# Dealing 90 adaLN steps differently over a two-layer hybrid block

## The chip, the core and the metric

The kernel runs on one core of a Trainium2 chip. Its engines go by the profile's names: PE multiplies matrices (PEld loads its weights), DVE, ACT and POOL do elementwise work, SP issues all transfers from HBM. The metric is the device time of one execution in microseconds, as the median of several runs. All arithmetic is float32; products are made from a high and a low float32r part of both operands, in three matmuls.

## The reference

Two layers over 256 latent tokens and 256 context tokens of width 1024. Per layer six adaLN vectors of 1024 (shift, scale and gate for the mixer, then for the feed forward) are products of a conditioning vector with a 1024 x 6144 matrix, one set per stream:

```python
mod_x = (jax.nn.silu(c) @ w_ada[l] + b_ada[l])[:, None, :]
mod_c = (jax.nn.silu(c_ctx) @ w_ada[l] + b_ada[l])[None, None, :]
shift1, scale1, gate1, shift2, scale2, gate2 = jnp.split(mod_x, 6, axis=-1)
...
hx = modulate(x, shift1, scale1)          # LN(x) * (1 + scale) + shift
mix_x, _ = token_mixer(hx, *mixer_w, rope, ctx_kv)
x = layer_norm(alpha * x + gate1 * mix_x, ln1_g[l], ln1_b[l])
ffn_x = swiglu(modulate(x, shift2, scale2), w_up[l], w_down[l])
x = layer_norm(alpha * x + gate2 * ffn_x, ln2_g[l], ln2_b[l])
```

The mixer is attention, a gMLP and a Fourier branch, merged under three sigmoid gates (`merged = sum of gate_b * (branch_b @ P_b)`) and multiplied with `w_out`. The last layer needs its context stream for keys and values alone, so of its context vectors only shift1 and scale1.

## The kernel before, in words

**Order of the work.** The code does not issue instructions itself. Every operation is appended to a plan in program order (its rank). Buffers are then given out in program order, each from a ring of its class: 7 `raw` tiles of 128x1024 for arriving weights, 3 `whi` and 3 `wlo` for their two parts, 34 `A` tiles, 8 PSUM banks. Last, a list scheduler with costs and latencies written into the code (`cost`, `LATENCY`) puts the operations of each engine in a fixed order: an engine that is free takes the ready operation of lowest rank. On the chip every engine goes through its own list strictly in order and waits where the next operation is not ready.

**A weight tile.** `load_w` transfers 512 KB into a `raw` tile, ACT copies it to `whi` (rounded), DVE subtracts it to get `wlo`; a resident tile goes to `A` tiles instead (`rhi`, `rlo`). The raw tile is free after the subtraction.

**An adaLN step.** `ada_queue` holds closures; `ada_step(n)` takes the next n. A tile step (`ada_tile`) loads 128 columns of `w_ada` (512 KB, one raw tile) and for each stream issues one DVE SCALAR_TENSOR_TENSOR (tile `junkv`) that multiplies by the broadcast conditioning row and sums into one column of `mod`; a small accumulator read follows. A group of six per layer (0 shift1, 1 scale1, 2 gate1, 3 shift2, 4 scale2, 5 gate2) is eight tile steps and one `fin` step (`ada_fin`), which adds the bias. For gates 2 and 5 `fin` also transposes on PE (`gtp`), copies on ACT (`grw`) and writes the gate to DRAM, from where it is read back as a broadcast row (`grow`).

**The stages.** Layer 0 carries both streams, 512 tokens. In the mixer the blocks of `w_in` come first (`zp`), with attention in the background; then for each of eight feature tiles j the three gates (`gp`, three weight tiles, 72 matmuls) of tile j+1 and the merge (`bp`, two weight tiles, 48 matmuls) of tile j, and after each merge some adaLN steps and, in the last layer, `after_merge`, which preloads `w_out`. Then `w_out` (`pj`), normalisations, the feed forward's up projection (`up`, feature tiles j = 0 to 21: the first three by `up_tile`, the rest by `up_seven`, a Strassen-like scheme with seven products of 12 matmuls), the down projection (`proj_streams`, k = 0 to 21, adaLN steps after each of the first 16), and layer 1 with 256 tokens in the same order, with `w_up_tok` (`ut`) at the start of its up projection.

**up_seven.** Each j takes two raw tiles for its weights and two more (`upy`, `upz`) for sums that DVE makes. DVE also evacuates the products; among these `nc.vector.tensor_tensor(f[:, 0], f[:, 0], a, op=ALU.subtract)` (tile `upf`) reads bank `a`, into which the next product `t4` accumulates.

**Who needs what when.** Layer 0's groups 2 to 5 are used in layer 0 after the merges. Layer 1's groups 0 and 1 are used when layer 1 begins, group 2 after its merges, 3 and 4 in its `mod`, 5 at the end. Before, 36 steps lay in layer 0's merges (5 each for four, 4 each for four), 26 in the down projection (2 each for ten, 1 each for six), 28 in layer 1's merges (4 each for four, 3 each for four). The queue has 32 tile steps of layer 0 with two streams, 16 of layer 1 with two (groups 0, 1), and 32 of layer 1 with one.

Of the kernel before, what the change touches and what calls it, by code (L numbers as in the profile page):

```python
# [39 lines left out]
RATE = [0.38, 0.5]  # L40

KEEP = 5

SPARE = 24

# [261 lines left out]
class Builder:  # L307
# [208 lines left out]
        else:  # L516
            nc.vector.tensor_tensor(m, m, b, op=ALU.add)

    def ada_enqueue(self, l, g, streams):
        for j in range(8):  # L520
            self.ada_queue.append(lambda j=j: self.ada_tile(l, g * 8 + j, streams))
        def fin():
            for s in streams:
                self.ada_fin(l, g, s)
        self.ada_queue.append(fin)

    def ada_step(self, n=1):
        for _ in range(n):
# [524 lines left out]
    def mixer(self, l, hx, hx_tiles, hc, early, pre=None, after={}, after_merge=None):  # L1053

        nc, io = self.nc, self.io
        both = l == 0
        streams = [0, 1] if both else [0]
# [114 lines left out]
        own, g = {}, []  # L1172
# [13 lines left out]
        for j in range(8):  # L1186
            if j < 7:
                self.gates(l, j + 1, hx, N, g, own)
                self.bg_drain()
            if j % 2 == 0:  # L1190
                for s in streams:
                    o, ts = self.feats(2, 256, f"mT{s}{j}")
                    mT[s] += o
                    mt[s] += ts
            self.merge(l, j, [g.pop(0) for _ in range(3)], own, A["aT"], gT, fT, N, [mT[s][j] for s in streams])
            self.ada_step((5 if both else 4) if j < 4 else (4 if both else 3))
            if after_merge:
                after_merge(j)
        return mT, mt
# [5 lines left out]
    def run(self):  # L1205
# [84 lines left out]

        for g in (2, 3, 4, 5):
            self.ada_enqueue(0, g, [0, 1])
        for g in (0, 1):
            self.ada_enqueue(1, g, [0, 1])
        for g in (2, 5, 3, 4):
            self.ada_enqueue(1, g, [0])


        mT, mt = self.mixer(0, hT, ht, None, early, pre)
# [20 lines left out]
        for s in range(2):  # L1320
            y = ys[s]
            done = lambda i, b: y.__setitem__(i, self.gated(b, grow[s]))
            if s == 0:
                held = self.proj_pair(io["w_out"][0], range(KD), mT[0], done, range(KD - KEEP, KD))
            else:
                order = [(k - KEEP) % KD for k in range(KD)]
                self.proj_pair(io["w_out"][0], order, mT[1], done, (), held, during_ctx)
# [6 lines left out]
        def hid_alloc(j):  # L1334
            if j % 2 == 0:
                t = self.a_tile([128, 2, 2, 2, 128], F32, f"hid{j}")
                hid.extend(t[:, i] for i in range(2))
# [11 lines left out]
        for j in range(NH, KF):  # L1349
            hid_alloc(j)  # L1350
            self.up_seven(j, h2, S, hid[j])

        ln = self.ln_rows(0, 1)
        hn, hnt = [None, None], [None, None]
# [3 lines left out]
        def down_done(s, i, b):  # L1358
# [4 lines left out]
            if (s, i) == (1, 0):  # L1363
# [1 line left out]
                self.modulated(y[0], 1, 0, 0, hn[0], 0)  # L1365

        self.proj_streams(io["w_down"][0], KF, hid, down_done, 6,
                          lambda k: self.ada_step(2 if k < 10 else 1))


        def ctx_in():
# [156 lines left out]
```

## Time and profile before

| | |
|---|---|
| time, median of 3 runs | 1324.29 us (1322.74 to 1325.91) |
| profiled execution, its own time | 1327.01 us |
| its span, first to last instruction | 1325.2 us |
| mean granted PE clock | 0.991 |
| adaLN tile steps | 128 instructions of 1233 ns on DVE, 157.8 us |

Shares are of the span. PE's busy time is modelled from the length of each matmul, so that a matmul that waits for nothing can still come more slowly; the pace (start to start) says more. The granted clock is a share of 2.4 GHz.

### The profile page before, as it was taken

How to read it: one execution, taken by the hardware profiler on the slowest of the kernel's cores; microseconds unless marked ns; L12 is line 12 of the kernel's file. 1: busy time of each engine (PE TensorE's matmuls, PEld its weight loads, DVE VectorE, ACT ScalarE, POOL GpSimd, SP SyncE). 2: the span in 40 equal slices, each digit the busy share in tenths (PEclk: the TensorE clock that was granted, in tenths of full speed). 3: DMA queues.
4: the chain of work that ended last, by engine and by line, in shares of the span. 5: the costliest groups of instructions: out<-in, count | busy, mean ns of one | idle time of the engine just before them, and what ended most of it. 6: DMA issues, size and time to landing. Idle time of an engine off the chain costs nothing.

```text
span 1325.2 us, 20495 instructions
## 1 busy us (share of the span) xinstructions
PE 1299.6 (98%) x7878; PEld 1150.5 (87%) x7878; DVE 1020.7 (77%) x1878; ACT 608.2 (46%) x1080; POOL 96.2 (7%) x99
## 2 busy tenths in 40 slices
PE   9999999999999999999999999999999899999997
PEld 8887888888888889999999888878899897799985
DVE  6867886876786679688989996786987787766665
ACT  4456564332222446455556323564754453444450
POOL 0032100000100111000000000242000001100000
PEclk8999999999999999999999999999999899999999
DMA  9611115445455730133336786044257795555551
GB/s 367 238 48 48 48 60 160 143 142 175 160 184 182 286 127 33 49 98 111 112 99 221 259 281 237 27 145 138 89 179 246 260 331 209 178 187 184 187 191 48
DMA packets 60819, 214.29 MB, mean 162 GB/s; under 512 B 7297, under 2 KB 8113, under 8 KB 60721
## 3 DMA queue, kind: packets, MB, share of 16 engines
q1 hardware_dynamic: 60720, 212.98, 47.9%
q8 instruction: 62, 1.02, 0.3%
q14 instruction: 37, 0.30, 0.1%
HBM read 211.88 MB, written 1.07 MB: 161 GB/s over the span
## 4 chain that ended last, share of the span: by engine, by line
PE 85%; DVE 6%; DMA 4%; ACT 2%; issue 2%; POOL 0%; SPq 0%; DVEq 0%; ACTq 0%; POOLq 0%
PE up L295 24%; PE pj L295 18%; PE zp L295 15%; PE gp L295 11%; PE bp L295 7%; DMA raw<-in_w_ada_t 3%; PE pvp L295 2%; PE sp L295 2%; PE tpp L295 1%; DVE junkv L295 1%; PE adp L295 1%; PE ut L295 1%; DVE wlo L295 1%; PE trp L295 1%; DMA raw<-in_w_out 1%
## 5 line engine op out<-in xcount | busy, mean ns | idle before, releaser
L295 ACT ACTIVATE whi<-raw 128x1024 fp32r<-128x1024 f32 x216 | 228.5, 1060 | 345.6 <-issue 97.3
L295 DVE TENSOR_TENSOR wlo<-raw,whi 128x1024 fp32r<-128x1024 f32 x216 | 264.2, 1225 | 132.7 <-ACT whi L295 132.2
L295 DVE SCALAR_TENSOR_TENSOR junkv<-raw,silb 128x1024 bf16<-128x1024 f32 x128 | 157.8, 1233 | 32.0 <-DMA raw<-in_w_ada_t 30.5
L295 PE MATMUL up<-h,whi 128*128 128x256 f32 x880 | 155.2, 281 | 0.0
L295 PEld LDWEIGHTS up<-h,whi 128*128 128x128 f32 x880 | 133.8, 189 | 0.2
L295 PE MATMUL up<-h,wlo 128*128 128x256 f32 x440 | 120.6, 281 | 0.0
L295 PE MATMUL gp<-hT,whi 128*128 128x512 f32 x384 | 120.3, 394 | 0.0
L295 PE MATMUL zp<-whi,hT 128*128 128x512 f32 x320 | 111.7, 404 | 0.1
L295 PEld LDWEIGHTS gp<-hT,whi 128*128 128x128 f32 x384 | 71.6, 188 | 15.4
L295 PEld LDWEIGHTS up<-h,wlo 128*128 128x128 f32 x440 | 81.6, 188 | 0.0
L295 PE MATMUL pj<-whi,hidp 128*128 128x512 f32 x256 | 79.8, 392 | 0.0
L295 PE MATMUL gp<-hT,wlo 128*128 128x512 f32 x192 | 75.7, 394 | 0.0
L295 PE MATMUL gp<-hx,whi 128*128 128x256 f32 x384 | 73.5, 290 | 2.0 <-ACT whi L295 2.0
L295 PEld LDWEIGHTS zp<-whi,hT 128*128 128x128 f32 x320 | 60.2, 190 | 12.0 <-DVE hT L295 0.5
L295 ACT ACTIVATE rhi<-raw 128x1024 fp32r<-128x1024 f32 x44 | 45.6, 1054 | 47.2 <-DMA raw<-in_w_out 19.8
L295 PE MATMUL zp<-whi,hx 128*128 128x512 f32 x192 | 66.1, 407 | 0.2 <-ACT moda L295 0.2
L295 DVE TENSOR_TENSOR rlo<-raw,rhi 128x1024 fp32r<-128x1024 f32 x44 | 54.5, 1246 | 14.7 <-ACT rhi L295 14.6
L295 PEld LDWEIGHTS gp<-hx,whi 128*128 128x128 f32 x384 | 61.9, 197 | 2.4 <-ACT whi L295 2.2
L295 PE MATMUL zp<-wlo,hT 128*128 128x512 f32 x160 | 63.3, 397 | 0.0
L295 PE MATMUL bp<-aT,whi 128*128 128x512 f32 (+1 forms) x256 | 63.1, 338 | 0.0
L295 PE MATMUL gp<-hx,wlo 128*128 128x256 f32 x192 | 55.6, 290 | 1.9 <-DVE wlo L295 1.9
L295 POOL TENSOR_TENSOR gth<-gth 128x512 f32<-128x512 f32 (+1 forms) x16 | 24.2, 1510 | 455.7 <-DVE gth L295 302.1
(291 smaller groups left out, 3165.5 us busy)
## 6 DMA issues: line engine op xcount, KB each, us to landing
raw<-in_w_ada_t SPq DMA_DIRECT2D x80, 512.0 KB, 4.4
raw<-in_w_up SPq DMA_DIRECT2D x80, 512.0 KB, 3.7
raw<-in_w_in_tok SPq DMA_DIRECT2D x48, 512.0 KB, 4.0
raw<-in_w_gate SPq DMA_DIRECT2D x48, 512.0 KB, 4.4
raw<-in_w_down SPq DMA_DIRECT2D x44, 512.0 KB, 3.9
raw<-in_w_br SPq DMA_DIRECT2D x32, 512.0 KB, 3.7
raw<-in_w_out SPq DMA_DIRECT2D x19, 512.0 KB, 5.9
wsh<-in_w_ada_s SPq DMA_DIRECT2D x8, 512.0 KB, 10.7
```

Source lines behind the costliest of these rows:

```text
L295: getattr(getattr(nc, eng), method)(*map(real, args), **{k: real(a) for k, a in kw.items()})
```

## The change

Steps move; their number (90) and the work of each stay. `ADA_MERGE` gives layer 0's merges 6,6,6,6,6,5,5,5 steps (45) and layer 1's 2,2,1,1,1,1,1,1 (10). A step is added after every odd j of `up_seven` from 3 to 17 (8), and the down projection has 27. The queue is put in another order: layer 1's group 0 goes to the end of layer 0's merges; the eight tiles of its group 2 go to the feed forward, without their `fin`; groups 1, 3 and 4 go to the down projection; `fin` of group 2 stays the first step of layer 1's merges, and group 5 follows it.

```diff
+ADA_MERGE = [[6, 6, 6, 6, 6, 5, 5, 5], [2, 2, 1, 1, 1, 1, 1, 1]]
...
-    def ada_enqueue(self, l, g, streams):
-        for j in range(8):
-            self.ada_queue.append(lambda j=j: self.ada_tile(l, g * 8 + j, streams))
-        def fin():
-            for s in streams:
-                self.ada_fin(l, g, s)
-        self.ada_queue.append(fin)
+    def ada_enqueue(self, l, g, streams, tiles=True, fin=True):
+        if tiles:
+            for j in range(8):
+                self.ada_queue.append(lambda j=j: self.ada_tile(l, g * 8 + j, streams))
+        if fin:
+            self.ada_queue.append(lambda: [self.ada_fin(l, g, s) for s in streams])
...
-            self.ada_step((5 if both else 4) if j < 4 else (4 if both else 3))
+            self.ada_step(ADA_MERGE[l][j])
...
-        for g in (0, 1):
-            self.ada_enqueue(1, g, [0, 1])
-        for g in (2, 5, 3, 4):
+        self.ada_enqueue(1, 0, [0, 1])
+        self.ada_enqueue(1, 2, [0], fin=False)
+        self.ada_enqueue(1, 1, [0, 1])
+        for g in (3, 4):
             self.ada_enqueue(1, g, [0])
+        self.ada_enqueue(1, 2, [0], tiles=False)
+        self.ada_enqueue(1, 5, [0])
...
             self.up_seven(j, h2, S, hid[j])
+            self.ada_step(j % 2 if j < 19 else 0)
...
-                          lambda k: self.ada_step(2 if k < 10 else 1))
+                          lambda k: self.ada_step(2 if k < 11 else 1))
```

## Rows read from the trace of the kernel before

**Rows 1.** The page: span, then busy us, share and instructions of two engines.
```profile
span 1325.2 us, 20495 instructions
PE 1299.6 (98%) x7878; PEld 1150.5 (87%) x7878; DVE 1020.7 (77%) x1878; ACT 608.2 (46%) x1080; POOL 96.2 (7%) x99
```

**Rows 2.** Stages: length; busy PE, PEld, DVE, ACT, POOL (instructions); clock; DMA share; GB/s.
```profile
281.00:458.50 177.50, 177.50 (x774) 144.33 (x773) 123.29 (x183) 52.84 (x72) 12.11 (x7) 1.00 0.58 195
498.50:525.00 26.50, 25.94 (x195) 24.14 (x193) 25.83 (x60) 17.86 (x32) 4.25 (x4) 1.00 0.12 41
525.00:731.00 206.00, 205.93 (x1741) 205.58 (x1741) 179.57 (x316) 112.73 (x192) 0.00 (x0) 1.00 0.35 115
731.00:849.00 118.00, 118.00 (x523) 96.38 (x522) 97.27 (x154) 39.70 (x51) 5.05 (x5) 1.00 0.63 210
996.00:1103.17 107.17, 101.15 (x824) 100.20 (x823) 82.34 (x118) 49.20 (x68) 6.99 (x7) 0.97 0.84 290
1126.00:1142.00 16.00, 13.97 (x64) 10.08 (x63) 15.12 (x40) 10.03 (x21) 3.33 (x2) 1.00 0.48 153
```

**Rows 3.** Layer 1's merges in stretches of about one period.
```profile
1010.70:1024.90 14.20, 14.20 (x123) 14.20 (x122) 11.73 (x19) 6.53 (x9) 0.74 (x1) 1.00 0.89 310
1024.90:1039.00 14.10, 12.68 (x108) 12.45 (x107) 8.66 (x14) 6.57 (x10) 0.74 (x1) 1.00 0.73 250
1039.00:1053.00 14.00, 11.45 (x82) 10.94 (x81) 9.15 (x13) 4.40 (x5) 1.65 (x1) 0.85 0.79 259
1053.00:1067.00 14.00, 14.00 (x110) 14.00 (x110) 11.63 (x18) 6.60 (x10) 0.41 (x1) 0.90 0.89 306
1095.00:1103.10 8.10, 6.06 (x51) 5.85 (x51) 5.54 (x9) 2.83 (x4) 1.65 (x1) 1.00 0.93 355
```

**Rows 4.** The same stage, merge matmuls alone, then gate matmuls alone.
```profile
996.40:1103.10 106.70, 46.72 (x384) 45.83 (x384) 8.57 (x21) 0.97 0.84 292
996.40:1103.10 106.70, 55.86 (x434) 54.34 (x432) 6.92 (x19) 0.97 0.84 292
```

**Rows 5.** Timeline of PE there: start, us, operation, [idle before, releaser]; rows with idle.
```profile
1038.16 0.39 PE L295 MATMUL gp<-hx,wlo 128*128 128x256 f32 x1 [1.43 <-DVE wlo L295]
1048.75 0.74 PE L295 MATMUL gp<-hx,whi 128*128 128x256 f32 x2 [2.03 <-ACT whi L295]
1050.01 0.58 PE L295 MATMUL gp<-hx,wlo 128*128 128x256 f32 x1 [0.52 <-DVE wlo L295]
1100.32 0.39 PE L295 MATMUL bp<-gT,wlo 128*128 128x256 f32 x1 [2.04 <-DVE wlo L295]
```

**Rows 6.** Chain of waits there: start, us, what the chain ran through.
```profile
1022.45 5.46 DMA raw<-in_w_ada_t
1040.41 7.13 DMA raw<-in_w_gate
1091.16 6.30 DMA raw<-in_w_ada_t
```

**Rows 7.** Waits, 968 to 1103 us: total us, times, longest us.
```profile
DVE junkv L295 <- DMA raw<-in_w_ada_t: 15.1, 13, 3.8
```

**Rows 8.** Timeline of DVE around one adaLN tile.
```profile
1006.29 1.23 DVE L295 SCALAR_TENSOR_TENSOR junkv<-raw,silb 128x1024 bf16<-128x1024 f32 x1
1007.44 0.08 DVE L295 DVE_READ_ACCUMULATOR junkv<-raw,silb 128x1 f32 x1
1007.44 1.22 DVE L295 TENSOR_TENSOR wlo<-raw,whi 128x1024 fp32r<-128x1024 f32 x1
```

**Rows 9.** Timeline in the feed forward, DVE rows, then one of PE.
```profile
605.29 0.68 DVE L295 TENSOR_TENSOR wf<-raw,wf 128x512 fp32r<-128x512 f32 x1
607.04 1.22 DVE L295 TENSOR_TENSOR wlo<-raw,whi 128x1024 fp32r<-128x1024 f32 x1 [1.06 <-ACT whi L295]
609.64 0.41 DVE L295 TENSOR_TENSOR upf<-upf,up 128x256 f32<-128x256 f32 x1
...
610.12 0.64 PE L295 MATMUL up<-h,whi 128*128 128x256 f32 x4
```

## The prediction

> **What bounds the kernel now.** I read the page first, then busy time by stage, then the stage that stood out by period, its gaps on PE, its chain of waits, and last the DVE timelines of the places that get the steps. The page says that PE is busy for 1299.6 of 1325.2 us [rows 1]: whatever is to be won is PE's idle time, or matmuls that come too slowly though PE counts as busy. By stage PE has no idle time in layer 0's merges and in the down projection, 0.07 us in the feed forward, and 6.0 us in layer 1's merges (107.17 less 101.15), the only one of them with a granted clock under 1.00, and with the highest DMA share, 0.84 [rows 2]. So these merges are bound by something other than PE, and the other three by PE.
>
> **How much is lost in layer 1's merges.** Of the eight periods of this stage the second is clean: 14.20 us, PE busy throughout, clock 1.00 [rows 3]. A period is 72 gate and 48 merge matmuls. The stage holds 384 merge matmuls and 434 in gates, two of which belong to the edge [rows 4]: 816, or 6.8 periods, which at 14.20 us take 96.6 us. It took 106.7 us. The loss is 10.1 us. Most of it can be named: four gaps of 1.43, 2.03, 0.52 and 2.04 us, 6.0 us [rows 5], and two stretches of 14 us at a granted clock of 0.85 and 0.90, thus partly at 1.2 in place of 2.4 GHz, which is worth 14 x 0.15 + 14 x 0.10 = 3.5 us [rows 3]. Within this stage the clock fell after the gaps, and only there.
>
> **Why there are gaps.** The chain runs from transfer to transfer, mostly through adaLN tiles, of 4.5 to 6.3 us each, of which two stand in the rows [rows 6]; DVE stood still 13 times for such a tile, 15.1 us, up to 3.8 us [rows 7], and the wlo subtractions that PE needs stand behind it in DVE's list. A period transfers five weight tiles, three or four adaLN tiles and, from j = 3, one of w_out: nine or ten of 512 KB (0.524 MB), or 332 to 369 GB/s at a period of 14.2 us. The stretches show 250 to 355 GB/s [rows 3]. The seven raw tiles turn too slowly for that.
>
> **What the change takes out there.** Eight adaLN tiles stay of 24. A period then transfers six or seven tiles, 222 to 258 GB/s; the clean period was fed at 310 [rows 3]. For the whole stage: 290 GB/s over 107.17 us is 31.1 MB, less 16 x 0.524 leaves 22.7 MB, 235 GB/s over 96.6 us. DVE goes from 82.3 us [rows 2] by 16 x 1.15 (start to start of an adaLN instruction and the next operation [rows 8]) to 63.9 of 96.6 us. So PE becomes the bound: -10.1 us. One gap like those of 2.04 us may stay somewhere; between 0 and 2.0 I take 0.3, since the clean period is the nearest row. The Trainium skill (Perfetto Trace Analysis, Identifying the Most-Contended Engine, with the table of Engine Utilization) judges transfers by their rate against 358 GB/s per core. By it this stage, at 290 GB/s or 81%, is not bound by transfers and nothing is freed, and the sum would be 1325.3 us; the last stretch, at 355 GB/s with PE idle for 2.04 us [rows 3], speaks against it for the peaks, if not for the mean. It is the third rival below.
>
> **Layer 0's merges** get nine steps more: eight tiles with two streams and one fin, that is eight transfers and 16 x 1.15 = 18.4 us on DVE. In the stretch shown DVE goes from 123.3 to at most 141.7 of 177.5 us, 80%, and transfers from 195 by 4.2 MB / 177.5 us to 219 GB/s [rows 2]. Layer 1's clean period had DVE at 83% and 310 GB/s while PE missed nothing [rows 3], so I take 0. It cannot gain, as PE has no idle time there. The upper end is a gap of 2.0 us [rows 5], at its tail above all, where one tile more stands ahead of w_out and the normalisations, and the stretch behind already has 0.56 us of PE idle with DVE at 25.83 of 26.50 us [rows 2]. Group 5's fins move ahead, from the last step of these merges to the first after j = 6: nobody waits for them there.
>
> **The feed forward** gets eight tiles with one stream, one in each second j. DVE is nearly full there: 179.6 of 206 us [rows 2]. In the steady state of 9.9 us per j (84 matmuls at 206 / 1741 = 0.118 us [rows 2]) DVE has one gap of 1.06 us, ahead of the first wlo of the next j, while ACT waits for PE to give a whi tile back [rows 9]. A tile takes 1.15 us [rows 8]. Over two j that is 17.7 + 1.15 = 18.8 of 19.8 us, so it fits. The scheduler gives DVE the ready operation of lowest rank; the tile's rank is above all of its own j and below the next j, so it comes when nothing of its j is ready: in the gap. It overfills it by 0.09 us. What follows is the subtraction upf, whose end at 610.05 us frees the bank that PE's next product goes into at 610.12 [rows 9]: no cover to speak of, and 8 x 0.09 = 0.7 us. If the tile stands ahead of upf instead, each costs PE its whole 1.15 us, 9.2 us in all. The ends are 0 and 9.2; I take 0.7, because the gap is the nearest row. Its transfer joins a stage at 115 GB/s [rows 2]. One more raw tile in the ring makes the next weights start up to one tile later; they feed sums that DVE can make up to a gap later.
>
> **The down projection** has 27 steps for 26, but 24 tiles as before, now eight with two streams and 16 with one for 16 and eight: 32 instructions for 40, 9.2 us less on DVE. PE is full for all 118 us [rows 2]: 0. **The rest:** the fin of gate 2 stays the first step of layer 1's merges. The fin of gate 5 goes from the third merge to the end of the last, with its transpose just ahead of w_out; its last tile lies a merge earlier, so 0, and 2.0 us at most if DVE is late. Behind the merges PE is idle for 2.0 us (16.00 less 13.97), with DVE at 15.12 of 16 us [rows 2]: splits of w_up_tok between normalisations. Weights that come earlier could give up to these 2.0 us; the A tiles decide when they may be split, so 0.
>
> **Sum.** -10.1 + 0.3 + 0.7 = -9.1 us. The profiled execution took 1327.01 us, 1.8 us around its span, and would take 1317.9. The median of the runs is 2.7 us below it, 1324.29, and I put the difference there: 1315.2 us.
>
> **Rivals.**
> First, the weights stay late by themselves. The longest gap, 2.03 + 0.52 us, came behind a gate's transfer of 7.13 us [rows 6], not an adaLN tile's. If that gap and the lower clock after it stay (2.55 + 3.5 = 6.05 us), the sum is -3.1: 1321.2 us. For it: that row, and w_out's tiles, which come from j = 3 on as before. Against: the transfer was long because of what shared the engines with it.
> Second, slower. DVE goes in order, and a tile in the feed forward that is not there when its turn comes stops the subtractions behind it. Priced as in layer 1's merges, a wait of 15.1 / 13 = 1.16 us [rows 7] and 1.15 of work, ahead of upf, are 2.3 us of PE for each of eight steps, 18.5 us, against 10.1: +8.4, 1332.7 us. It decides from 10.1 / 8 = 1.26 us per step. For it: the gap is smaller than the tile, and upf has no cover. Against: at a DMA share of 0.35 [rows 2] a transfer started a j ahead lands in time.
> Third, transfers do not bind, and the gaps are of another origin, such as the three whi tiles: the loss stays, only the feed forward's 0.7 is added, about 1325. For it: a mean DMA share of 0.84, not 1. Against: the clean period has the same three whi tiles and no gap.
>
> **Chances.** Forecast 0.66, first rival 0.16, slower 0.11, nothing 0.07. A measurement of this kernel can tell about 0.2%, 2.6 us, from no change; both of the first two lie beyond it. Faster 0.82, within 0.2% 0.07, slower 0.11. The range: below, all 10.1 us and 2 more behind the merges, with nothing lost, 1312; above, the first rival and a little, 1322. Outside lie the third rival, the second, and little else. The likeliest case alone would lie between 1312 and 1318.
>
> **What would show it.** Right: layer 1's merges take 96 to 98 us at a clock of 1.00 and about 235 GB/s; DVE's waits for adaLN tiles fall from 15.1 to a few us; the feed forward keeps its 206 us within 1 us, with the tile in the 1.06 us gap; layer 0's merges and the down projection keep 177.5 and 118 us. Wrong: PE gaps in the feed forward behind upf; a gap in layer 1's merges behind a gate's transfer; PE gaps around 458 to 525 us.

## The result and the profile after

| | before | after |
|---|---|---|
| median of 4 runs each, us | 1324.41 (1322.74 to 1325.91) | 1312.87 (1311.66 to 1315.59) |
| ratio after/before | | 0.9916 [0.9896, 0.9936] |
| profiled execution, its time and span, us | 1327.01, 1325.2 | 1312.18, 1310.4 |

The change makes the kernel faster by 0.84%, 11.5 us between the medians, 8.5 to 13.8 us by the interval. The forecast was 9.1 us less, 1315.2 us.

The page after, beside [rows 1]: the span, then PE and the other engines as there.

```profile
span 1310.4 us, 20491 instructions
PE 1290.6 (98%) x7878; PEld 1143.0 (87%) x7878; DVE 1017.2 (78%) x1878; ACT 606.7 (46%) x1080; POOL 97.9 (7%) x99
```

The shares have hardly moved; they could not have told where the time was. The stages of [rows 2], in the same columns (length; busy PE, PEld, DVE, ACT, POOL; clock; DMA share; GB/s), do:

```profile
276.40:454.00 177.60, 177.60 (x773) 144.36 (x772) 137.75 (x211) 53.00 (x73) 12.58 (x7) 1.00 0.66 216
494.00:520.40 26.40, 25.84 (x195) 24.04 (x193) 25.86 (x60) 17.88 (x32) 4.26 (x4) 1.00 0.09 24
520.40:727.00 206.60, 206.14 (x1740) 205.60 (x1741) 188.70 (x334) 111.22 (x192) 0.00 (x0) 1.00 0.40 134
727.00:845.00 118.00, 118.00 (x523) 96.32 (x522) 87.66 (x136) 39.82 (x51) 5.04 (x5) 1.00 0.61 211
991.68:1088.30 96.62, 96.62 (x819) 96.58 (x818) 69.38 (x93) 49.08 (x67) 8.81 (x8) 1.00 0.80 267
1111.20:1127.20 16.00, 14.01 (x64) 10.09 (x63) 15.11 (x40) 10.04 (x21) 3.32 (x2) 1.00 0.44 147
```

Layer 1's merges (fifth row) went from 107.17 to 96.62 us, PE busy in all of it, clock 1.00. Every other stage in these rows kept its length within 0.6 us, although DVE does more in the first row (137.75 for 123.29) and the third (188.70 for 179.57), and less in the fourth (87.66 for 97.27).

The chain of waits in layer 1's merges (start, us, what the chain ran through) had transfers of 5 to 7 us in it [rows 6]. After, it never leaves PE from the first merge to `w_out`:

```profile
991.68 5.69 PE bp L297 x48
997.37 0.11 PE gtp L297
997.48 8.50 PE gp L297 x72
1005.98 5.68 PE bp L297 x48
1011.66 8.51 PE gp L297 x72
...
1068.43 8.57 PE gp L297 x72
1077.00 11.37 PE bp L297 x96
1088.37 0.11 PE gtp L297
1088.47 11.27 PE pj L297 x48
```

Each pair of 48 and 72 matmuls takes 14.19 us, the pace of the clean period [rows 3]. DVE's waits from 963 to 1089 us (total us, times, longest), beside [rows 7]:

```profile
DVE wlo L297 <- ACT whi L297: 16.1, 16, 2.0
...
DVE junkv L297 <- DMA raw<-in_w_ada_t: 3.9, 2, 3.1
```

Waits for adaLN transfers fell from 15.1 to 3.9 us. DVE now waits for ACT, which costs nothing, because PE is the bound.

**Where the 14.8 us between the two profiled spans lie.** By the starts of PE's first and last matmuls of each kind: the stretch from layer 1's last input product to the last `w_out` matmul (called S below) went from 164.46 to 155.22 us, -9.2; layer 0's gates, first to last, from 214.82 to 213.48, -1.3; the Strassen part of the feed forward from 179.4 to 180.0, +0.6. Two parts are chance: the start, up to layer 0's last input product, took 3.1 us less with its order unchanged (its mean granted clock was 0.98 before and 0.99 after), and layer 1's input products 1.6 us less, because the profile of before has a spell at a clock of 0.50 from 881.6 to 885.0 us. The two chance parts are why the profiles differ by more than the medians.

### The profile page after: what moved, and what is told of

The parts are those of the page before. It is cut to its first block, busy times and chain, and to the rows that moved or that the text cites. A ratio compares the mean times of both kernels' runs of the same rounds, so it can differ in the third digit from the quotient of the medians.

```text
span 1310.4 us, 20491 instructions
## 1 busy us (share of the span) xinstructions
PE 1290.6 (98%) x7878; PEld 1143.0 (87%) x7878; DVE 1017.2 (78%) x1878; ACT 606.7 (46%) x1080; POOL 97.9 (7%) x99
## 3 DMA queue, kind: packets, MB, share of 16 engines
HBM read 211.88 MB, written 1.07 MB: 163 GB/s over the span
## 4 chain that ended last, share of the span: by engine, by line
PE 90%; DVE 5%; ACT 2%; DMA 1%; issue 1%; POOL 0%; SPq 0%; DVEq 0%; ACTq 0%; POOLq 0%
PE up L297 22%; PE pj L297 18%; PE gp L297 15%; PE zp L297 15%; PE bp L297 10%; PE pvp L297 2%; PE sp L297 2%; PE tpp L297 1%; PE ut L297 1%; PE trp L297 1%; DVE wlo L297 1%; PE adp L297 1%; DMA raw<-in_w_up 1%; PE fop L297 1%; ACT junka L297 1%
## 5 line engine op out<-in xcount | busy, mean ns | idle before, releaser
L297 PE MATMUL gp<-hx,whi 128*128 128x256 f32 x384 | 70.5, 283 | 0.0
L297 DVE TENSOR_TENSOR rlo<-raw,rhi 128x1024 fp32r<-128x1024 f32 x44 | 53.5, 1219 | 15.1 <-ACT rhi L297 14.5
L297 PEld LDWEIGHTS pj<-whi,hidp 128*128 128x128 f32 x256 | 48.1, 188 | 10.6
```

The costliest lines, as they stand in the source:

```text
L297: getattr(getattr(nc, eng), method)(*map(real, args), **{k: real(a) for k, a in kw.items()})
```

## Experiments

Ratios are to the kernel before, measured beside each run (its medians there: 1325.24, 1325.85 and 1325.31 us). "Merges" runs from the first merge matmul of layer 1 to the first of `w_out`, in one profile each; in e11 that first `w_out` matmul lies among the merge matmuls, so the column stays empty. Every kernel gets its static order anew, so an edit also moves other instructions.

| run | us | ratio | merges | S |
|---|---|---|---|---|
| before | 1324.41 | 1 | 106.6 | 164.5 |
| after | 1312.87 | 0.9916 [0.9896, 0.9936] | 96.7 | 155.2 |
| e1 DVE work back | 1318.48 | 0.9943 [0.9928, 0.9958] | 99.5 | 158.5 |
| e2 transfers back, DVE reads a column | 1325.51 | 1.0001 [0.9987, 1.0014] | 105.1 | 163.6 |
| e3 transfers back, nobody reads | 1319.58 | 0.9958 [0.9942, 0.9975] | 99.2 | 159.4 |
| e4 before, eight raw tiles | 1323.94 | 0.9996 [0.9983, 1.0009] | 104.4 | 164.0 |
| e5 no feed-forward tiles | 1316.19 | 0.9937 [0.9914, 0.9960] | 96.5 | 155.0 |
| e6 twice the feed-forward tiles | 1315.28 | 0.9935 [0.9917, 0.9953] | 96.7 | 155.2 |
| e7 layer 0's part alone | 1316.17 | 0.9943 [0.9926, 0.9960] | 100.0 | 158.3 |
| e8 feed forward's part alone | 1320.63 | 0.9970 [0.9957, 0.9983] | 99.9 | 158.9 |
| e9 16 small loads, DVE reads | 1315.99 | 0.9939 [0.9924, 0.9953] | 96.7 | 155.1 |
| e10 transfers back, POOL reads | 1320.62 | 0.9961 [0.9948, 0.9974] | 103.9 | 161.8 |
| e11 before, planned for later landings | 1329.27 | 1.0040 [1.0026, 1.0055] | | 155.5 |
| e12 after, again | 1313.25 | 0.9919 [0.9905, 0.9934] | 96.9 | 155.4 |

**e1 to e4: what of the 16 tiles costs the time?** A tile is a transfer of 512 KB into a raw tile and DVE work on it. e1 gives layer 1's merges DVE's work back without transfers, e2 the transfers with a tiny read of each by DVE, e3 the transfers alone; their results are used by nobody. e4 is the kernel before with one raw tile more.

```diff
+EXTRA = [2, 2, 2, 3, 1, 2, 2, 2]          # per merge of layer 1
 # e1
+for _ in range(EXTRA[j] if l == 1 else 0):
+    ...
+    nc.vector.scalar_tensor_tensor(self.junk["v"], self.silb[0], last[:, 0:1], self.silb[1],
+                                   op0=ALU.mult, op1=ALU.add, accum_out=sm)
 # e2; e3 without the last line
+for i in range(EXTRA[j] if l == 1 else 0):
+    ...
+    nc.sync.dma_start(raw, io["w_ada_t"][0, 2 * j + i])
+    ...
+    nc.vector.tensor_copy(sm, raw[:, 0:1])
 # e4, in the kernel before
-CLASSES = {"A": 34, "raw": 7, ...
+CLASSES = {"A": 34, "raw": 8, ...
```

> The changed kernel with 16 DVE instructions more in layer 1's merges, of the size of an adaLN tile's (128x1024, with accumulator), on rows that are resident: the DVE work that the change took out is back, its 16 transfers are not. DVE would be busy there for about 69.4 + 16 x 1.15 = 88 of 96.6 us. Theory (transfers through seven raw buffers): layer 1's merges stay at 96.6 to 98 us without a gap on PE, time within 2 us of the changed kernel's 1312.9. First rival (DVE's work made the 10.1 us): the merges take 104 us or more, time near 1322. Second rival (DVE standing in order behind late tiles): as the theory.

> The changed kernel with 16 transfers of 512 KB more in layer 1's merges, each read by one DVE copy of a single column: the transfers and DVE's waits for them are back, DVE's 18 us of work are not. Theory (transfers): the merges take 103 to 107 us, with gaps on PE, about 290 GB/s, time 1319 to 1324. First rival (DVE's work): 97 to 98 us, time about 1313. Second rival (DVE standing behind late tiles): as the theory.

> The changed kernel with the same 16 transfers, read by nobody: a raw buffer is free again as soon as its transfer lands, and DVE never waits for one. Theory (the transfers and their seven buffers are the loss): 101 to 107 us for the merges, because the weights' transfers still queue behind 16 others, time 1317 to 1324. Second rival (the loss is DVE standing behind late tiles): 97 to 98 us, time about 1313. First rival (DVE's work): 97 to 98 us.

> The kernel before with eight raw buffers in place of seven, and nothing else. If the number of buffers sets the pace (seven tiles of 0.524 MB turned in 12.2 us at 300 GB/s), the pace rises by up to an eighth, from 1.75 to 1.53 us per tile against the 1.42 to 1.58 that PE asks for, and layer 1's merges fall from 106.6 to 97 to 101 us: time 1314 to 1319. If the transfer engines themselves set it (shares of 0.9 and more, 347 to 355 GB/s, in the late stretches), the merges stay within 2 us of 106.6, time 1322 to 1326. I expect something between, nearer the first.

The merges of e1, e2, e3 and e4, one row each:

```profile
995.04:1094.51 99.47, 97.49 (x821) 96.91 (x819) 82.69 (x117) 49.35 (x67) 7.87 (x7) 1.00 0.75 254
```

```profile
992.22:1097.28 105.06, 99.98 (x821) 98.48 (x819) 68.13 (x104) 49.66 (x69) 7.02 (x7) 0.99 0.86 304
```

```profile
991.42:1090.65 99.23, 97.19 (x821) 96.74 (x819) 67.41 (x90) 49.71 (x67) 6.10 (x7) 1.00 0.87 314
```

```profile
997.96:1102.38 104.42, 98.96 (x825) 97.53 (x823) 78.86 (x117) 49.27 (x72) 6.07 (x7) 1.00 0.84 285
```

Against the change (0.9918, the mean of after and e12) the times say: DVE's work alone +3.3 us, the transfers alone +5.3, the transfers with a tiny read by DVE +11.0, all that the change had won; the intervals make each of these uncertain by some 2 us. e4 falls flat, 0.9996: a ring of eight loses what the ring of seven does. The rows say where. In e1 DVE is as busy as in the kernel before, 82.69 us, and the merges take 99.5 us, not the 96.6 to 98 that were expected; e3 moves 314 GB/s, more than before's 292 in the same stretch, and PE still is busy for 97.19 of 99.23 us, with another 1.07 us of idle time at the start of `w_out`; its 99.2 us lie between what was expected of the transfers (101 and more) and of DVE's waiting (98 and less). One caution: the profile of e2 and that of e3 were taken in the fastest of their runs (1321.29 and 1316.15 us), so their rows show less than the medians. In e2 and e4 DVE waits for the transfers:

```profile
DVE exs L299 <- DMA raw<-in_w_ada_t: 15.4, 9, 4.1
...
DVE junkv L299 <- DMA raw<-in_w_ada_t: 5.2, 3, 3.0
```

```profile
DVE junkv L295 <- DMA raw<-in_w_ada_t: 20.3, 11, 5.3
```

In e1 there is next to nothing of it (2.9 us), yet a fuller DVE makes PE wait twice (PE's timeline; in brackets the idle time before and who ended it):

```profile
1039.19 0.39 PE L299 MATMUL bp<-aT,wlo 128*128 128x256 f32 x1 [0.77 <-DVE wlo L299]
...
1054.85 0.39 PE L299 MATMUL bp<-aT,wlo 128*128 128x256 f32 x1 [1.22 <-DVE wlo L299]
```

**e9 and e10: DVE's waiting, the ring, or the bytes?** e9 takes as many raw tiles and DVE reads as e2, but transfers 4 KB for each. e10 is e2 with POOL as the reader, so that DVE waits for none of the added tiles.

```diff
 # e9, in e2
-    nc.sync.dma_start(raw, io["w_ada_t"][0, 2 * j + i])
+    nc.sync.dma_start(raw[:, 0:8], io["w_ada_t"][0, 2 * j + i][:, 0:8])
 # e10, in e2
-    nc.vector.tensor_copy(sm, raw[:, 0:1])
+    nc.gpsimd.tensor_tensor(sm, raw[:, 0:1], self.mhalf[:, 0:1], op=ALU.add)
```

> The changed kernel with the 16 raw buffers more in layer 1's merges, each held until one DVE copy of a column has read it as in the load and copy run, but with transfers of 4 KB (128 x 8) in place of 512 KB. What is left of that run's loss (8.4 us over the changed kernel between the last input product and the last of w_out, 163.6 against 155.2 us) is due to buffers and DVE's order, what goes is due to the bytes. Theory as it stands after the run with eight buffers (the bytes, not the buffers): 155 to 157 us, time about 1313 to 1315. Rival (the ring of buffers): 160 us and more, time 1319 and up.

> The changed kernel with 16 transfers of 512 KB more, read by a POOL instruction of one column: buffers are held as in the load and copy run, but DVE does not wait for them. That run took 163.6 us in the stretch, the one in which nobody reads them 159.4. If the difference of 4.2 us is DVE standing in order behind late tiles: 159 to 160 us, time about 1318 to 1320. If it is the buffers being held until they are read: 162 to 164 us, time about 1323 to 1326.

Their merges, e9 first, then e10 and its waits:

```profile
995.78:1092.47 96.69, 96.69 (x821) 96.65 (x819) 68.72 (x104) 50.10 (x69) 7.02 (x7) 1.00 0.75 260
```

```profile
994.73:1098.64 103.91, 99.36 (x821) 98.25 (x819) 67.46 (x91) 49.84 (x69) 14.44 (x22) 0.99 0.86 307
```

```profile
POOL exs L299 <- DMA raw<-in_w_ada_t: 112.8, 15, 39.7
...
DVE junkv L299 <- DMA raw<-in_w_ada_t: 9.6, 4, 4.7
...
PE bp L299 <- DVE wlo L299: 4.1, 4, 1.8
```

Sixteen more turns of the ring and sixteen more DVE reads cost nothing in the merges when the transfers are small. By its times e9 is 2.8 us above the change, but so are e5 (2.6) and e6 (2.3), whose merges are as short: a difference of that size between medians is not yet a cost in this stage. So the bytes are necessary to e2's loss, and the number of raw tiles is not its cause. With POOL as the reader the 16 transfers cost +5.7 us, as in e3 with no reader at all (+5.3), and half of e2's +11.0: the other half goes with DVE, which goes in order, reading tiles that land late. POOL waits for them 112.8 us, and DVE waits for POOL's products no longer than after the change (1.6 and 1.3 us in the merges). The rows of the profiles put e10 (103.9 us of merges) nearer to e2; but e10 was profiled in its slowest run of nine, 1322.66 us, and e2 in its fastest of ten, so here the medians decide. The split into halves is therefore rough; that both parts are there is shown.

**e7 and e8: how much must go?** Each does half of the change, so that 16 of the 24 tiles stay in layer 1's merges: e7 moves the eight to layer 0's merges, e8 the eight to the feed forward (the queue's order follows; only the numbers of steps are shown).

```diff
 # e7: no steps in the feed forward, two after each k < 10 of the down projection
-ADA_MERGE = [[6, 6, 6, 6, 6, 5, 5, 5], [2, 2, 1, 1, 1, 1, 1, 1]]
+ADA_MERGE = [[6, 6, 6, 6, 6, 5, 5, 5], [3, 3, 3, 2, 2, 2, 2, 2]]
 # e8: steps in the feed forward kept, two after each k < 10
+ADA_MERGE = [[5, 5, 5, 5, 4, 4, 4, 4], [3, 3, 3, 3, 2, 2, 2, 2]]
```

> Only the layer 0 part of the change: 45 steps in layer 0's merges, none in the feed forward, 26 in the down projection, 19 in layer 1's merges (16 tiles, where before had 24 and the changed kernel 8). A period there transfers seven to eight tiles, 258 to 295 GB/s, under the 310 of the clean period. Theory (transfers): layer 1's merges take 97 to 100 us, most of the loss gone at two thirds of the tiles; layer 0's merges unchanged; time 1313 to 1317. Rival (the loss is in proportion to the tiles): half of it stays, 101.6 us, time about 1318.

> Only the feed forward part: 36 steps in layer 0's merges as before, 8 in the feed forward, 26 in the down projection, 20 in layer 1's merges (16 tiles). Theory: as the layer 0 part alone, 97 to 100 us for layer 1's merges, and 0.6 us more in the feed forward; time 1314 to 1317. The first gates and merges of layer 0 should show whether the 1.3 us that the changed kernel won there come from its order of steps (then they are not won here) or from chance.

Merges of 100.0 and 99.9 us: eight tiles fewer give 6.6 and 6.7 of 9.9 us, two thirds for half the tiles. That is more than in proportion, and less than the clean period's 310 GB/s as a threshold would give: both kernels stay under it and still lose 3.3 us. DVE's waits for adaLN tiles stayed long, 15.0 us in e7 and 22.2 us in e8, but fewer of them reached PE (2.7 and 2.6 us of gaps). The layer-0 half also brought layer 0's own 1.3 us (213.5 against 214.8 in e8), below. The times were expected alike; e8's, 1320.63 us, lies above its 1314 to 1317 and 3.6 us above e7's, which that 1.3 and the 0.6 of S explain only in part.

**e5 and e6: the feed forward.** e5 drops the eight tiles (gate1 of layer 1 is then its bias alone); e6 issues a tile in the even j too, 16 in all.

```diff
 # e5
-            self.ada_step(j % 2 if j < 19 else 0)
+            if j % 2 and j < 19:
+                self.ada_queue.pop(0)
+            ...
 # e6, added behind the step
+            if j % 2 == 0 and j < 19:
+                self.ada_tile(1, 16 + j // 2 - 2, [0])
```

> The changed kernel without the eight adaLN tiles in the feed forward; their sums are left out of the computation (gate1 of layer 1 is its bias alone). Layer 1's merges stay at 96.6 us. Theory (each tile overfills DVE's gap of 1.06 us by 0.09 us, and PE pays for that): the feed forward, from the first to the last product of the Strassen part, gets 0.6 to 0.7 us shorter, back to that of the kernel before (179.4 us), time 1311.5 to 1313. Rival (the 0.6 us are something else, such as another order of the first features): no change of the stage, 180.0 us.

> The changed kernel with a second tile per two features in the feed forward (16 for 8, the eight even ones done twice without a use): DVE then needs 8.85 + 1.15 = 10.0 us per feature against PE's 9.92. Theory (the gap takes one tile per feature but for 0.09 us): DVE becomes the bound by about 0.1 us per feature, the stage grows by 1 to 2.5 us over the changed kernel's 180.0. Rival (no cover ahead of the subtraction that PE waits for, so that a full DVE costs PE the whole tile): 8 x 1.15 us = 9 us and more, time 1322 and up.

Without the tiles the Strassen part takes 179.6 us and the kernel is no faster (0.9937, its interval holds 0.9916). With eight it takes 179.2 to 180.0 in seven of eight profiles, 180.9 in the other (e9); with 16, 180.6, about 1 us more. Kernels without a tile there spread as much (179.4 in before and e7, 180.7 in e11, 181.6 in e4), so the eight cost 0.2 us at the mean (179.65 against 179.47 in before, e5 and e7) and nothing that can be told from the spread. In e6 PE is kept waiting once:

```profile
616.07 0.39 PE L297 MATMUL up<-hs3h,whi 128*128 128x256 f32 x1 [0.95 <-ACT upe L297]
```

**e11: is it the bytes or the order?** Old transfers, old steps: the kernel before, but its scheduler believes that a 512 KB transfer lands after 5.75 us instead of 3.9. Measured in the merges of before, the median of an adaLN tile is 5.5 us.

```diff
-    LATENCY = {"tensor": 0.2, "vector": 0.15, "scalar": 0.14, "gpsimd": 0.1, "sync": 2.6}
+    LATENCY = {"tensor": 0.2, "vector": 0.15, "scalar": 0.14, "gpsimd": 0.1, "sync": 4.0}
-        return max(0.35, 128 * n * 4 / 400e3)
+        return max(0.35, 128 * n * 4 / 300e3)
```

> The kernel before, with nothing changed but what the scheduler believes of transfers: 300 in place of 400 GB/s and 4.0 in place of 2.6 us of latency, so that 512 KB land after 5.75 us (the traces show a median of 5.3 in layer 1's merges) and not 3.9. The order on every engine follows. If the loss is largely DVE and ACT standing behind tiles that the list expects too early, an order made for later landings wins a good part of it without moving a step: 157 to 161 us in the stretch from the last input product to the last of w_out, against 164.4 before. If the bytes bind: 163 to 166 us. Elsewhere the order may get worse, so the time itself says less: 1315 to 1330.

The 97 us from its first merge matmul on, and further behind 12 us in which `w_out` has ended:

```profile
1001.00:1098.00 97.00, 97.00 (x811) 96.66 (x810) 78.57 (x115) 46.46 (x65) 9.64 (x7) 1.00 0.85 292
```

```profile
1120.00:1132.00 12.00, 5.51 (x18) 4.09 (x17) 12.00 (x31) 8.30 (x15) 2.43 (x2) 0.72 0.42 142
```

With 28 steps in these merges, at the 292 GB/s of before, PE runs without a gap: S is 155.5 us, as after the change, and DVE waits for no transfer. Neither that rate nor 28 steps force the loss; the order of the lists decides, with what it leaves for later. Two things in it differ. The list reckons with 5.75 us between a request and its reader, and fewer weights of the next stage come along (issues in the merges: out<-in, count, KB each, median us to landing; e11, then before):

```profile
raw<-in_w_ada_t SPq DMA_DIRECT2D x19, 512.0 KB, 4.5
...
raw<-in_w_up_tok SPq DMA_DIRECT2D x2, 512.0 KB, 8.9
```

```profile
raw<-in_w_ada_t SPq DMA_DIRECT2D x19, 512.0 KB, 5.5
...
raw<-in_w_up_tok SPq DMA_DIRECT2D x5, 512.0 KB, 4.9
```

The win is given back behind: from the last `w_out` to the last `ut` matmul e11 takes 34.8 us in place of 27.9, with PE idle once for 5.40 us while DVE normalises, at a clock of 0.72; layer 0's feed forward and down projection together take 1.9 us more (350.8 for 349.0 us, from the first `up` matmul to layer 1's first input product). In total it is slower. How much of its clean merges comes from the longer lead and how much from the three `w_up_tok` tiles put off is not separated, and an order with late landings for the merges alone was not tried.

**e12** repeats the changed kernel beside e9 to e11.

> The changed kernel once more, beside the others on one chip. Ratio to before 0.990 to 0.993. Layer 1's merges at 96.6 us again. The feed forward's Strassen part, 180.0 us in the first profile and 179.4 before, should be 179.3 to 179.6 if the one gap of 0.39 us there was chance (three other runs with the same tiles had that), and 180.0 if the tiles cost it.

0.9919 [0.9905, 0.9934], merges 96.9 us, S 155.4, the Strassen part 179.4: the result stands, and the feed forward's 0.6 us in the first profile are no fixed cost.

## Why the prediction was right, point by point

**The loss in layer 1's merges, 10.1 us: size right, cause half right.** 96.6 us was forecast from the clean period, 96.62 measured in the stage row. From first merge matmul to `w_out` it is 9.9 us; 0.7 is lost again ahead of the merges (36.1 us after layer 1's last input product, for 35.4), so that S gains 9.2. The 0.3 kept for a gap that stays wasn't needed. The step that failed is the cause, "The seven raw tiles turn too slowly for that", with 332 to 369 GB/s as the measure. Two stretches of the same stage before, which [rows 3] leave out, already speak against it: PE has no gap in them at 347 and 325 GB/s.

```profile
1067.00:1081.00 14.00, 14.00 (x121) 14.00 (x120) 11.06 (x16) 7.30 (x10) 0.33 (x1) 1.00 0.96 347
1081.00:1095.00 14.00, 14.00 (x120) 14.00 (x119) 12.40 (x16) 8.20 (x11) 0.73 (x1) 1.00 0.94 325
```

Of the runs, e3 moves 314 GB/s with a loss of 2.5 us in its profile, e11 292 with none, and an eighth tile (e4) changes nothing. What the runs show in its place: by the medians about half of the cost is the 512 KB of each tile, with a reader off DVE or none (e3, e10), about half is DVE standing in its fixed order for tiles that are late (e2 against e10), and another order of the same steps avoids both in this stage, with three `w_up_tok` tiles fewer (e11). The shares are not sums of parts: DVE's work without transfers costs 3.3 us too (e1, by its time and by S). The lists were made for a landing after 3.9 us; it comes after 5.5 at the median.

That eight tiles were few enough was in part luck. The forecast's measure, a rate under the clean period's 310 GB/s, also holds for the 16 tiles of e7 and e8, and they lose 3.3 us. The lower clock, 3.5 us of the forecast's loss, went away with the gaps; gaps alone do not always bring it, as e4 has 5.46 us of PE idle (104.42 less 98.96) at a clock of 1.00.

**Bytes.** 235 GB/s forecast, 267 measured. Of the 24 tiles 19 were transferred within the stage before, and 6 of 8 after: 13 fewer, not 16. And seven of `w_up_tok`'s come there now instead of five. DVE's busy time missed in the same way, 69.4 us against 63.9. Neither changed the time: PE was busy in all of the 96.62 us.

**The third rival** had its premise right: transfers at 290 GB/s didn't bind as a rate. The Trainium skill (Perfetto Trace Analysis, Identifying the Most-Contended Engine, with Engine Utilization) judges transfers by their rate against 358 GB/s per core; 290 GB/s is 81% of it, by which they are not the bound, and e11's gapless 292 GB/s agrees. That the rate does not bind does not make the transfers free: unread, at 314 GB/s, 16 more still cost 5.3 us (e3). The rival's conclusion, that nothing is freed, does not follow: gaps behind transfers that come late for a fixed order go away when tiles go away.

**Layer 0's merges, 0: they gained 1.3 us ahead of the first merge.** The sentence "It cannot gain, as PE has no idle time there" was wrong. From the first gate matmul to the first merge matmul it takes 48.1 to 48.5 us in the old order (before, e4, e8, e11) and 46.9 to 47.0 in the ten profiles with the new one. The rows of [rows 2] begin at 281 us and missed the place. At 255 us in the profile of before (PE's timeline) single matmuls start 0.39, 0.39 and 0.51 us apart, at a full clock, two of them with no idle time on record:

```profile
254.81 0.39 PE L295 MATMUL gp<-hT,wlo 128*128 128x512 f32 x1
255.20 0.39 PE L295 MATMUL fpc<-foa,dc 128*128 128x260 f32 x1
255.59 0.30 PE L295 MATMUL sgt<-idn,u 128*128 128x128 f32 x1
256.10 0.51 PE L295 MATMUL fpc<-foa,dc 128*128 128x260 f32 x2 [0.20 <-DVE foa L295]
```

The weight loads (PEld) of the two `fpc` show what they wait for:

```profile
255.19 0.19 PEld L295 LDWEIGHTS fpc<-foa,dc 128*128 128x128 f32 x1 [0.42 <-ACT foa L295]
...
256.09 0.30 PEld L295 LDWEIGHTS fpc<-foa,dc 128*128 128x128 f32 x2 [0.40 <-DVE foa L295]
```

In the kernel after the gate matmuls of this place start 0.23 us apart and an `fpc` 0.12 us before the next. The lists differ there: PE has six gate matmuls between the last `fop` and that `fpc` where before it has three, and DVE makes `foa` ahead of an adaLN tile and not behind it (before, then after):

```profile
253.96 1.21 DVE L295 SCALAR_TENSOR_TENSOR junkv<-raw,silb 128x1024 bf16<-128x1024 f32 x1
...
255.37 0.67 DVE L295 TENSOR_TENSOR foa<-fop,foa 128x512 fp32r<-128x512 f32 x1
```

```profile
251.63 0.68 DVE L297 TENSOR_TENSOR foa<-fop,foa 128x512 fp32r<-128x512 f32 x1
252.23 1.21 DVE L297 SCALAR_TENSOR_TENSOR junkv<-raw,silb 128x1024 bf16<-128x1024 f32 x1
```

Which of the moved steps brought this order was not tried; e4 and e11 lose the time at other waits of the same stretch.

**The feed forward, 0.7 us: about 0.2.** The tile lies where it was forecast, in the gap of [rows 9] (DVE's timeline, then PE's next product behind upf):

```profile
591.40 1.21 DVE L297 SCALAR_TENSOR_TENSOR junkv<-raw,silb 128x1024 bf16<-128x1024 f32 x1
592.55 0.08 DVE L297 DVE_READ_ACCUMULATOR junkv<-raw,silb 128x1 f32 x1
...
593.15 1.21 DVE L297 TENSOR_TENSOR wlo<-raw,whi 128x1024 fp32r<-128x1024 f32 x1
...
595.75 0.41 DVE L297 TENSOR_TENSOR upf<-upf,up 128x256 f32<-128x256 f32 x1
...
603.03 1.23 DVE L297 TENSOR_TENSOR wlo<-raw,whi 128x1024 fp32r<-128x1024 f32 x1 [1.06 <-ACT whi L297]
```

```profile
596.22 0.63 PE L297 MATMUL up<-h,whi 128*128 128x256 f32 x4
```

The tile fills one gap, and the next j has its gap of 1.06 us again. upf follows wlo by 2.60 us as in [rows 9], and wlo came 9.88 us before the next one, a j at PE's pace. So the second rival, 2.3 us for each of eight steps, did not happen; even 16 tiles cost 1 us and not 18. One PE gap behind upf, which the forecast named as a sign of being wrong, does stand in the profile after, two j earlier:

```profile
576.55 0.50 PE L297 MATMUL up<-h,whi 128*128 128x256 f32 x2 [0.39 <-DVE upf L297]
```

So the lack of cover that the forecast saw there is real; of the other seven profiles with eight tiles only e9 has such a gap (0.82 us), so it is not a fixed cost of a tile. The first rival, a gate's weights late by themselves, left no trace: PE has no gap in these merges after.

**Down projection and the rest, 0:** 118.00 us of PE in 118.00, and 1.99 us of idle time behind `w_out` as before (16.00 less 14.01).

**Sum.** -9.2 in S, -1.3 in layer 0 and about +0.2 in the feed forward are -10.3 us; -11.5 was measured, and the interval holds both it and the forecast's -9.1.

## What to carry to other kernels

Judge a stage by the pace of a clean period of its own (here 14.20 us for 120 matmuls), not by PE's busy share of 98%: it gave the size of the gain although the cause was not yet known. Where every engine follows a fixed list, compare the landing time that the list was made for (3.9 us) with the one measured under load (5.5 us) before blaming the rate of transfers or the number of buffers. Work that moved cost next to nothing where it fell into a gap measured on the engine that took it, with a gap of 1.06 us and work of 1.15 us.

## What the runs showed of the hardware that was not expected

The same 16 transfers cost 5.3 us unread, 5.7 with one column read by POOL, which has little else to do (14.44 us busy of 103.91), and 11.0 with one column read by DVE, whose list holds PE's weights too; each of these is uncertain by some 2 us. At 314 GB/s, the highest mean rate in these merges in any of the kernels, PE still was busy for 97.19 of 99.23 us. And matmuls that wait briefly need not show as idle: at 255 us before, two of the three long steps, 0.39 us each, where the kernel after takes 0.12 to 0.23, count as busy in PE's row, and the wait of 0.42 us for the `fpc` in them shows only at its weight load.
